# Hybrid Mamba-2 and attention trunk: y in 64-token pieces, group 0 turned off TensorE, and a softmax tail moved one group forward

## The chip, the cores and the metric

One core of one Trainium2 chip runs the kernel. The metric is device time in microseconds (us): the median over runs of the same program. A profiled execution shows what each engine of the core did: PE (TensorE matmuls) and PEld (its weight loads), DVE (VectorE), ACT (ScalarE), POOL (GpSimd) and SP, whose queue starts most DMAs. An "L" and a number is a line of the kernel.

## The reference

Two layers over 256 tokens of width 2048, each followed by a layer norm of the input (times a constant) plus the layer's output. The first layer is a Mamba-2 state-space mixer with 64 heads of 64 in 8 groups, the second a sliding-window attention with 32 query heads over 4 shared key/value heads. The part of the first layer that the change touches, cut from the reference:

```python
zxbcdt = x @ w_in                       # z, xbc, dt_raw
xbc = silu(causal_conv4(xbc) + conv_b)  # xs (64 heads of 64), bm and cm (8 groups of 128)
dt = softplus(dt_raw + dt_bias); a = -exp(a_log)
da_cum = cumsum(dt * a)                 # per head, over tokens
cb     = einsum("bcqgn,bcsgn->bgcqs", c, b)                        # C with B, per group
y_diag = einsum("bgcqs,bgrcqs,bcsgrp->bcqgrp", cb, exp(segsum(da)), xs * dt)
# (the reference cuts tokens into chunks of 128 and carries states between them)
y = y_diag + y_off + xs * d_skip
y = rmsnorm_per_group(y * silu(z)) * norm_w
out = y @ w_out
```

For query token q and earlier token s, the weight of a head is cb[q, s] times the exponential of the sum of da between s and q. In the attention layer, scores become weights by a softmax over the window with one sink per head, the weighted values are multiplied by silu(gate), and an output projection follows.

## The kernel before

**Weights.** All large products are in float32, split in two parts: `wr` is a weight tile from memory (128x1024, loaded through SP's queue into six buffers), ScalarE makes its high part `wh` (L178), VectorE the rest `wl` (L181), and TensorE multiplies three times, high by high, high by low, low by high. A block of 128 output columns for 256 tokens is 48 matmuls of 256 columns (L265); a piece of an output projection is 24 matmuls of 512 columns (L339). Four tiles each of `wh` and `wl` go round.

**Layer one.** `_sequence` sets the order of the input blocks, one block a step. A group g has ten blocks: B, C, four `xs` and four `z`. For group 0 three of the `z` come first, then B, C, the four `xs` and the last `z` (`BLOCKS0`, steps 0 to 9); steps 10 to 19 are group 1's in the plain order. After a block's product, ScalarE and VectorE do the convolution: `cv` by ScalarE (L508), three more taps by VectorE (L510), then tanh by ScalarE (L515) and a product by VectorE (L516), which gives `bt`, `ct` or `xs`. Output pieces of an earlier group lie between the blocks (`OUT_AT`). Tables (`plan`, `beside`, `between`, filled by `at`) say at which step every small operation is written; a scheduler with priorities may shift it, except what is pinned to the written order. Each engine then works its own list in order.

**A group's y.** Tokens stand on the partitions as the earlier token s, in two blocks c of 128. The heads are worked in two halves of four, hf.

- `load_decay` fetches the running sums of da for four heads (`rb`), copied to all partitions, by one DMA per half. `sum_decay` forms the differences: per head one ScalarE operation of 256 and one of 128 columns (L566), since the second token block needs only the later 128 queries. `exp_decay` takes the exponential of all 1536 columns (L573).
- `cb` multiplies B with C for the whole group in two matmuls (L607, L608), and VectorE masks the result (L609). `by_cb` multiplies the exponentials of a half by it (L614). This product is `e`.
- `xd` holds xs times dt with tokens on partitions. For groups 1 to 7 VectorE transposes xs in 32x32 blocks (`turn_xs`, L641), ScalarE copies the blocks to their places (`carry_xs`, 16 copies, L651) and VectorE multiplies by dt (`scale_xs`, L657). For group 0 `turn_first` does it: eight TensorE transposes (L625) and four VectorE products out of PSUM (L629).
- `ymm` (L659) forms y: 16 matmuls for a group, each over 128 tokens s, 64 rows of output and 256 or 128 queries. Two heads go to the two halves of the output rows. TensorE works each float32 matmul as two records in the trace, so there are 32 records per group. VectorE takes y out of PSUM (L675, L681), POOL multiplies by the gate (L686, `gate`).

**Layer two.** `B_ORDER` gives the order of the query blocks q, gate blocks g and output blocks o for the four key/value heads j. After each half h of a group's attention, `weigh` (L1252 to L1255: sums, reciprocal, product) and `turn_far` (a VectorE transpose `z`, L1262, then 16 ScalarE copies, L1281) turn the scores into weights. They are called `rest`: for the two halves listed in `BEHIND_HALF` they are put off, (1, 1) to a later point in the next attention half, and (3, 0) to behind the first gate `sg` of block g3 (`behind_gate`). All others run at once. The gate is ScalarE's tanh (L1185) and VectorE's product (L1186), which frees the PSUM tile of the gate block; four `mm` tiles of PSUM go round.

Of the kernel before, what the change touches and what calls it, by code (L numbers as in the profile page):

```python
# [17 lines left out]
P = 128  # L18
S = 256
# [51 lines left out]
NSM = 7  # L71
B_ORDER = [("q", 0), ("g", 0), ("q", 1), ("g", 1), ("q", 2), ("o", 0), ("g", 2), ("q", 3),
# [6 lines left out]
BEHIND_HALF = [(1, 1), (3, 0)]  # L79
# [18 lines left out]
def trunk(ctx: ExitStack, tc: tile.TileContext, A: dict, out: bass.AP, dbg=None):  # L98
# [30 lines left out]
    mask_ssd = cc[:, 256:640]  # L129

    tri = cc[:, 256:384]
# [60 lines left out]
    def load_first():  # L192

        us = [new_unit([WHOLE, WHOLE]) for _ in range(NF)]
        raws = []
        for tag, n in FIRST:
            if tag == "xr":
                buf = xr_t
            elif tag == "wr":
                buf = wp.tile([P, 1024], F32, tag="wr", name=nm("first"), bufs=NR)  # L200
            else:
                w, bufs = {"rb": (1024, 2), "e": (1536, 2), "yz": (1024, 1)}[tag]
# [211 lines left out]
    dtx = ap.tile([P, 2, NHD], F32, tag="dtx", name="dtx")  # L414
    rtk = ap.tile([P, 2, 2 * NHD], F32, tag="rtk", name="rtk")
# [68 lines left out]
    def turn_dt(sums, dt, q):  # L484
        pt = ax_tile()
        for i, v in enumerate((sums[:, 0, :], sums[:, 1, :], dt)):
            nc.tensor.transpose(pt[:, i * P : (i + 1) * P], v, ident)
        nc.scalar.copy(
            rtk[:].rearrange("p c (k h) -> p k c h", k=2),
            pt[:, :256].rearrange("p (k c h) -> p k c h", k=2, c=2),  # L490
        )
        elo = q[:]
        nc.scalar.activation(
            elo[:, :128].rearrange("p (c h) -> p c h", c=2), rtk[:, :, 64:128], AF.Exp, scale=-1.0
        )
        nc.vector.tensor_tensor(
            dtx[:], pt[:, 256:384].rearrange("p (c h) -> p c h", c=2),
            elo[:, :128].rearrange("p (c h) -> p c h", c=2), ALU.mult,
# [30 lines left out]
    def load_decay(g, hf):  # L529
        rb = ap.tile([P, 4, S], F32, tag="rb", name=nm("rb"), bufs=2)  # L530
# [3 lines left out]
        m = (nc.sync if sp else nc.gpsimd).dma_start(  # L534
            rb[:],
            rscr[h0 : h0 + 4, :]
            .rearrange("h q -> (h q)").partition_broadcast(P)
            .rearrange("p (h q) -> p h q", h=4),
        )
        if sp and g < 2:  # L540
            tc.keep_in_program_order(m)
        rbs[g, hf] = rb
# [13 lines left out]
    def sum_decay(g, hf, first=0, last=4):  # L556

        rb = rbs[g, hf]
        h0 = g * 8 + hf * 4
        if first == 0:  # L560
            es[g, hf] = ap.tile([P, 4, 384], F32, tag="e", name=nm("e"), bufs=2)
        e = es[g, hf]
        for h in range(first, last):
            for c, cols in ((0, slice(0, 256)), (1, slice(256, 384))):
# [6 lines left out]
    def exp_decay(g, hf):  # L571
        e = es[g, hf]
        m = nc.scalar.activation(e[:], e[:], AF.Exp, scale=-1.0)  # L573
# [29 lines left out]
    def cb(g):  # L603
        st = gs[g]
        cbm = ap.tile([P, 384], F32, tag="cbm", name=nm("cbm"), bufs=1)
        ps = ax_tile()
        nc.tensor.matmul(ps[:, :256], st.bt[:, :128], st.ct[:], start=True, stop=True)  # L607
        nc.tensor.matmul(ps[:, 256:384], st.bt[:, 128:], st.ct[:, 128:], start=True, stop=True)  # L608
        nc.vector.tensor_tensor(cbm[:], ps[:, :384], mask_ssd, ALU.mult)  # L609
        st.cbm = cbm  # L610

    def by_cb(g, hf):
        e = es[g, hf]
        nc.vector.tensor_tensor(e[:], e[:], gs[g].cbm[:].unsqueeze(1).to_broadcast([P, 4, 384]), ALU.mult)  # L614

    def turn_first(g):

        st = gs[g]
        st.xd = ap.tile([P, 2, 4, P], F32, tag="xd", name=nm("xd"), bufs=1)
        for k in range(2):  # L620
            ps = ax_tile()
            for i in (2 * k, 2 * k + 1):
                for c in range(2):
                    o = (i % 2) * S + c * P
                    nc.tensor.transpose(ps[:, o : o + P], st.xs[i][:, c * P : (c + 1) * P], ident)  # L625
            for i in (2 * k, 2 * k + 1):
                o = (i % 2) * S
                hh = g * 8 + 2 * i
                m = nc.vector.tensor_tensor(  # L629
                    st.xd[:, :, i, :].rearrange("p c (h d) -> p c h d", h=2),  # L630
                    ps[:, o : o + S].rearrange("p (c h d) -> p c h d", c=2, h=2),
                    dtx[:, :, hh : hh + 2].unsqueeze(3).to_broadcast([P, 2, 2, 64]), ALU.mult,
                )
                pinned(m, True)

    def turn_xs(g):
# [3 lines left out]
        for i in range(4):  # L640
            m = nc.vector.transpose(st.zx[:, i].rearrange("p f b -> p (f b)"), st.xs[i][:])  # L641
            pinned(m, g == 1)
        st.xd = ap.tile([P, 2, 4, P], F32, tag="xd", name=nm("xd"), bufs=1)

    def carry_xs(g, js):

        st = gs[g]
        z = st.zx[:].rearrange("p i (c j) b -> p j c i b", c=2)
        for j in js:
            for i in range(4):  # L650
                m = nc.scalar.copy(st.xd[32 * j : 32 * j + 32, :, :, 32 * i : 32 * i + 32], z[32 * i : 32 * i + 32, j])  # L651
                pinned(m, g > 1 and j > 1)

    def scale_xs(g):
        v = gs[g].xd[:].rearrange("p c i (h d) -> p c (i h) d", h=2)
        d = dtx[:, :, g * 8 : g * 8 + 8].unsqueeze(3).to_broadcast([P, 2, 8, 64])
        pinned(nc.vector.tensor_tensor(v, v, d, ALU.mult), g == 0)  # L657

    def ymm(g):  # L659
        st = gs[g]  # L660
        st.yz = ap.tile([P, 4, S], F32, tag="yz", name=nm("yz"), bufs=1)
        for k in range(2):
            ps = ax_tile()
            for i in (2 * k, 2 * k + 1):
                o = (i % 2) * S
                for c in range(2):
                    cols = slice(o + c * P, o + S)
                    for r in range(2):
                        e = es[g, i // 2][:, 2 * (i % 2) + r, :]
                        nc.tensor.matmul(  # L670
                            ps[64 * r : 64 * r + 64, cols], st.xd[:, c, i, 64 * r : 64 * r + 64], e[:, 256:] if c else e[:, :256],
                            start=c == 0, stop=c == 1,
                        )
            two = slice(2 * k, 2 * k + 2)
            nc.vector.tensor_tensor(  # L675
                st.yz[:, two, :], ps[:].rearrange("p (i q) -> p i q", i=2), els[g][:, two, :], ALU.mult
            )
            for i in (2 * k, 2 * k + 1):
# [90 lines left out]
    visits = (turn_dt, cb, turn_first, ymm, norm)  # L769
# [89 lines left out]
    for g in range(NG):  # L859
        t = FIRST_XS[g]  # L860
        if g == 0:
# [5 lines left out]
            between[11] = [(turn_first, 0)]  # L867
# [55 lines left out]
        for i in range(4):  # L923
# [269 lines left out]
    def attend(j, h):  # L1193
# [172 lines left out]
        if (j, h) in BEHIND_HALF:  # L1366
            (behind_gate if j == 3 else halves).append(rest)
# [120 lines left out]
def _layout(inputs):  # L1488
# [61 lines left out]
    cc[:, 256:384] = tri  # L1550
    cc[:, 384:512] = 1.0
    cc[:, 512:640] = tri
# [31 lines left out]
```

## Time and profile before

| | |
|---|---|
| device time, median of 3 runs | 975.44 us (975.06 to 976.07) |
| profiled execution: time, and its span | 975.83 us, 973.8 us |
| PE busy | 965.5 us (99%) |
| DVE busy | 786.6 us (81%) |
| ACT busy | 671.4 us (69%) |
| POOL busy | 119.1 us (12%) |
| granted TensorE clock | 1.00 in every stretch |

The span is the time from the first to the last record; 2.03 us of the profiled execution lie outside it. Busy shares are averages over the whole span. A group's mean duration is that of one instruction, and neighbours on an engine can overlap by up to a tenth of a microsecond, so that the distance from start to start is shorter than a duration.

### The profile page before, as it was taken

To read this page: it belongs to the slowest core of one execution; us is meant where nothing else is said; L and a number is where in the kernel's file an instruction comes from. 1 tells how busy PE (TensorE), PEld (TensorE's weight loads), DVE (VectorE), ACT (ScalarE), POOL (GpSimd) and SP (SyncE) were. 2 spreads that over 40 slices of the span, in tenths; PEclk is the share of its full clock that TensorE was granted. 3 is DMA by queue.
4 is the path that set the end of the run, shared out by engine and by line. 5 is a ranking of instruction groups with operands and counts; after the bars stand their busy time and mean duration, and the time that the engine had idled before them with its cause. 6 is when DMAs were issued, how large, how long until landed. Compare 5 with 4: busy or idle time off the path is not lost.

```text
span 973.8 us, 18857 instructions
## 1 busy us (share of the span) xinstructions
PE 965.5 (99%) x7332; PEld 892.0 (92%) x7332; DVE 786.6 (81%) x1217; ACT 671.4 (69%) x1282; POOL 119.1 (12%) x202
## 2 busy tenths in 40 slices
PE   9999999999999999999999999999999999999998
PEld 8999989998999999999899899888999988898976
DVE  7978898896977877787797687889977769778778
ACT  7675884884785686487477579467777776884772
POOL 0000403102110310310300121411000000000002
PEclk9999999999999999999999999999999999999999
DMA  9689467676656666576476654568654545456542
GB/s 359 237 290 337 147 216 228 212 230 203 218 192 220 205 205 206 167 237 213 152 250 203 216 178 155 187 190 265 193 174 158 185 138 186 153 177 213 205 143 86
DMA packets 61273, 197.90 MB, mean 203 GB/s; under 512 B 6800, under 2 KB 11328, under 8 KB 60928
## 3 DMA queue, kind: packets, MB, share of 16 engines
q1 hardware_dynamic: 58528, 188.53, 59.1%
q0 software_dynamic: 2048, 7.65, 2.4%
q8 instruction: 57, 0.93, 0.4%
q10 hardware_dynamic: 608, 0.52, 0.2%
q14 instruction: 32, 0.26, 0.1%
HBM read 194.45 MB, written 2.23 MB: 202 GB/s over the span
## 4 chain that ended last, share of the span: by engine, by line
PE 75%; DVE 10%; ACT 6%; DMA 5%; issue 3%; SPq 1%; DVEq 0%; ACTq 0%
PE mm L265 48%; PE mm L339 20%; DVE wl L181 4%; DMA wr<-in_wa 2%; PE mm L1052 2%; PE ax L670 2%; ACT wh L178 2%; DMA wr<-in_wb 1%; ACT p L1248 1%; DMA xr<-in_first 1%; DVE cv L510 1%; ACT e L566 1%; ACT ptw L1281 1%; ACT pt L1281 0%; DMA rscr<-f 0%
## 5 line engine op out<-in xcount | busy, mean ns | idle before, releaser
L181 DVE TENSOR_TENSOR wl<-wr,wh 128x1024 fp32r<-128x1024 f32 (+2 forms) x354 | 391.5, 1126 | 87.8 <-ACT wh L178 86.0
L178 ACT ACTIVATE wh<-wr 128x1024 fp32r<-128x1024 f32 (+2 forms) x354 | 332.9, 974 | 95.9 <-PE mm L265 50.9
L265 PE MATMUL mm<-xH,wh 128*128 128x256 f32 x1280 | 354.6, 277 | 0.1
L265 PE MATMUL mm<-xH,wl 128*128 128x256 f32 x1280 | 353.8, 276 | 0.0
L265 PE MATMUL mm<-xL,wh 128*128 128x256 f32 x1280 | 353.7, 276 | 0.0
L265 PEld LDWEIGHTS mm<-xH,wh 128*128 128x128 f32 x1280 | 240.3, 188 | 2.3 <-issue 1.0
L265 PEld LDWEIGHTS mm<-xL,wh 128*128 128x128 f32 x1280 | 240.4, 188 | 1.0
L265 PEld LDWEIGHTS mm<-xH,wl 128*128 128x128 f32 x1280 | 240.3, 188 | 0.1
L265 PE MATMUL mm<-x1H,wh 128*128 128x256 f32 x512 | 142.2, 278 | 2.1 <-DVE sg L1186 2.1
L265 PE MATMUL mm<-x1L,wh 128*128 128x256 f32 x512 | 141.6, 277 | 0.0
L265 PE MATMUL mm<-x1H,wl 128*128 128x256 f32 x512 | 141.5, 276 | 0.0
L339 PE MATMUL mm<-wh,yH 128*128 128x512 f32 x256 | 100.8, 394 | 0.1
L339 PE MATMUL mm<-wh,yL 128*128 128x512 f32 x256 | 99.8, 390 | 0.0
L339 PE MATMUL mm<-wl,yH 128*128 128x512 f32 x256 | 99.7, 390 | 0.0
L265 PEld LDWEIGHTS mm<-x1H,wh 128*128 128x128 f32 x512 | 96.1, 188 | 3.6 <-DVE sg L1186 2.4
L265 PEld LDWEIGHTS mm<-x1L,wh 128*128 128x128 f32 x512 | 96.2, 188 | 0.1
L265 PEld LDWEIGHTS mm<-x1H,wl 128*128 128x128 f32 x512 | 96.2, 188 | 0.0
L510 DVE SCALAR_TENSOR_TENSOR cv<-mm,pc,cv 128x255 f32<-128x255 f32 x144 | 68.4, 476 | 4.6 <-ACT cv L508 2.5
L686 POOL TENSOR_TENSOR yz<-yz,z 128x256 f32<-128x256 f32 x32 | 26.7, 843 | 259.2 <-DVE yz L681 259.2
L339 PEld LDWEIGHTS mm<-wl,yH 128*128 128x128 f32 x256 | 48.1, 188 | 10.3
L339 PEld LDWEIGHTS mm<-wh,yH 128*128 128x128 f32 x256 | 48.1, 188 | 9.7 <-issue 0.3
L339 PEld LDWEIGHTS mm<-wh,yL 128*128 128x128 f32 x256 | 48.1, 188 | 9.0
(247 smaller groups left out, 1262.8 us busy)
## 6 DMA issues: line engine op xcount, KB each, us to landing
wr<-in_wa SPq DMA_DIRECT2D x154, 512.0 KB, 5.2
wr<-in_wo SPq DMA_DIRECT2D x64, 512.0 KB, 4.4
wr<-in_wq SPq DMA_DIRECT2D x32, 512.0 KB, 4.4
wr<-in_wg SPq DMA_DIRECT2D x31, 512.0 KB, 4.8
wr<-in_wb SPq DMA_DIRECT2D x16, 512.0 KB, 4.0
wr<-in_wb SPq DMA_DIRECT2D x32, 256.0 KB, 4.3
rb<-rscr SPq DMA_DIRECT2D x11, 512.0 KB, 5.4
wr<-in_wkv SPq DMA_DIRECT2D x8, 512.0 KB, 5.7
```

The lines of the kernel that those rows point to most:

```text
L178: m = nc.scalar.activation(h[:, sl], v, AF.Copy)
L181: m = nc.vector.tensor_tensor(l[:, sl], v, h[:, sl].bitcast(F32), ALU.subtract)
L265: m = nc.tensor.matmul(ps, a, b, start=first and i == 0, stop=last and i == 2)
L339: pinned(nc.tensor.matmul(ps, a[:, k, hs], (u.h, u.l)[l][:, ks], start=n == 0 and add is None, stop=n == 11), pin)
L510: nc.vector.scalar_tensor_tensor(a[:, sft:], ps[:, : S - sft], w(3 - sft), a[:, sft:], ALU.mult, ALU.add)
L566: m = nc.scalar.activation(e[:, h, cols], rb[:, h, c * P :], AF.Relu, scale=-1.0, bias=rtk[:, c, h0 + h : h0 + h + 1])
L670: nc.tensor.matmul(ps[64 * r : 64 * r + 64, cols], st.xd[:, c, i, 64 * r : 64 * r + 64], e[:, 256:] if c else e[:, :256], start=c == 0, st ...
L686: nc.gpsimd.tensor_tensor(v, v, st.z[i][:], ALU.mult)
L1052: m = nc.tensor.matmul(ps[:], (x1H, x1L, x1H)[i][:, kk, hs], (u.h, u.h, u.l)[i][:, ks], start=(kk, i) == (0, 0), stop=ui == 3 and (k, i) = ...
L1248: nc.scalar.activation(byhead[:, r], byhead[:, r], AF.Exp, bias=ng[:, r : r + 1], accum_out=rs[:, r : r + 1])
L1281: nc.scalar.copy(to[32 * c : 32 * c + 32].rearrange("p r a -> p (r a)"), src[32 * i : 32 * i + 32, cc_].rearrange("p r b -> p (r b)"),)
```

## The change

**The y product in 64-token pieces.** A group's earlier tokens are now cut in four pieces of 64. For piece c only queries from 64c on are needed, so the widths are 256, 192, 128 and 64 (`PART` gives their places in `e`). Tokens of one piece stand on half of the partitions: row half r holds one set of heads and the other half another, and b chooses the half of the output rows. `ymm` issues 32 matmuls, each over 64 tokens and 64 output rows, in sets of four that use the four quadrants of the array. `e` has 1280 columns for a half in place of 1536, and its PSUM tiles are one per row half. `cb` becomes four matmuls of 256, 192, 128 and 64 columns into output row halves, VectorE masks them in two operations of 64x320, and POOL copies both to the other half of the partitions (two copies more). `load_decay` fetches only the two heads that a row half needs: two DMAs of half the size for each before, in a buffer of their own kind; `sum_decay` has still 16 operations per group, of 256, 192, 128 and 64 columns; `turn_dt` copies in four pieces.

```diff
-        nc.tensor.matmul(ps[:, :256], st.bt[:, :128], st.ct[:], start=True, stop=True)
-        nc.tensor.matmul(ps[:, 256:384], st.bt[:, 128:], st.ct[:, 128:], start=True, stop=True)
-        nc.vector.tensor_tensor(cbm[:], ps[:, :384], mask_ssd, ALU.mult)
+        for c, half, to in ((0, 0, 0), (1, 64, 0), (2, 64, 192), (3, 0, 256)):
+            nc.tensor.matmul(
+                ps[half : half + 64, to : to + 256 - 64 * c], st.bt[:, 64 * c : 64 * c + 64], st.ct[:, 64 * c :],
+                start=True, stop=True,
+            )
+        for r in range(2):
+            rows, at = slice(64 * r, 64 * r + 64), slice(320 * r, 320 * r + 320)
+            nc.vector.tensor_tensor(cbm[rows, at], ps[rows, :320], mask_ssd[rows], ALU.mult)
+        for r in range(2):
+            ...
+            nc.gpsimd.tensor_copy(cbm[64 - 64 * r : 128 - 64 * r, at], cbm[rows, at])
...
     def ymm(g):
...
+        pss = [ax_tile(), ax_tile()]
         for k in range(2):
-            ps = ax_tile()
-            for i in (2 * k, 2 * k + 1):
-                o = (i % 2) * S
-                for c in range(2):
-                    cols = slice(o + c * P, o + S)
-                    for r in range(2):
-                        e = es[g, i // 2][:, 2 * (i % 2) + r, :]
+            for c in range(4):
+                for r in range(2):
+                    rows = slice(64 * r, 64 * r + 64)
+                    for b in range(2):
                         nc.tensor.matmul(
-                            ps[64 * r : 64 * r + 64, cols], st.xd[:, c, i, 64 * r : 64 * r + 64], e[:, 256:] if c else e[:, :256],
-                            start=c == 0, stop=c == 1,
+                            pss[r][64 * b : 64 * b + 64, k * S + 64 * c : k * S + S], st.xd[rows, k, b, c],
+                            es[g, k][rows, b, PART[c]], start=c == 0, stop=c == 3,
                         )
...
     def load_decay(g, hf):
-        rb = ap.tile([P, 4, S], F32, tag="rb", name=nm("rb"), bufs=2)
+        rb = ap.tile([P, 2, 2, S], F32, tag="rb", name=nm("rb"), bufs=2)
...
+        for r in range(2):
+            m = (nc.sync if sp else nc.gpsimd).dma_start(
+                rb[64 * r : 64 * r + 64, 0],
...
     def sum_decay(g, hf, first=0, last=4):
...
+            for c in range(4):
                 m = nc.scalar.activation(
-                    e[:, h, cols], rb[:, h, c * P :], AF.Relu, scale=-1.0, bias=rtk[:, c, h0 + h : h0 + h + 1]
+                    e[:, b, PART[c]], rbs[g, hf][:, b, 64 * c :], AF.Relu, scale=-1.0,
+                    bias=rtk[:, c % 2, 0, c // 2, n : n + 1],
```

**Group 0's xs.** `turn_first` is gone. `turn_xs`, `carry_xs` and `scale_xs` do for group 0 what they do for the others, at steps 9, 10 and 11; `ymm` of group 0 stays behind step 13. The gates of a group go in the order 0, 2, 1, 3.

```diff
-            between[11] = [(turn_first, 0)]
+            at(9, turn_xs, 0)
+            at(10, carry_xs, 0, (0, 1))
+            at(11, carry_xs, 0, (2, 3))
+            at(11, scale_xs, 0)
...
-        for i in range(4):
+        for i in (0, 2, 1, 3):
             at(y, gate, g, i)
```

On ScalarE, group 0's exponentials (`e` in place), the block of B of group 1 (`bt`) and the weights of the steps after it stand like this before:

```order
L573 ACTIVATE e_871<-e_871 128x1536
L178 ACTIVATE wh_1091<-wr_1095 128x1024
L178 ACTIVATE wh_1173<-wr_1175 128x1024
L508 ACTIVATE cv_1079<-mm_1029,pc 128x256
L178 ACTIVATE wh_1173<-wr_1177 128x1024
L515 ACTIVATE bt_1078<-cv_1079 128x256
L178 ACTIVATE wh_1241<-wr_1243 128x1024
```

And after the change:

```order
L571 ACTIVATE e_876<-e_876 128x1280
L638 COPY xd_1032<-zx_1027 32x2x4x32 x8
L505 ACTIVATE cv_1095<-mm_1045,pc 128x256
L178 ACTIVATE wh_1117<-wr_1121 128x1024
L638 COPY xd_1032<-zx_1027 32x2x4x32 x6
L512 ACTIVATE bt_1094<-cv_1095 128x256
L638 COPY xd_1032<-zx_1027 32x2x4x32 x2
L178 ACTIVATE wh_1193<-wr_1195 128x1024
L178 ACTIVATE wh_1193<-wr_1197 128x1024
```

Sixteen copies now stand ahead of the weights for the next steps. On VectorE the products that make group 0's `xd` stand behind `bt` of group 1 and ahead of the block of `ct` before:

```order
L516 SCALAR_TENSOR_TENSOR bt_1078<-bt_1078,cv_1079 128x256
L629 TENSOR_TENSOR xd_1150<-ax_1151,dtx 128x2x128 x2
L629 TENSOR_TENSOR xd_1150<-ax_1158,dtx 128x2x128 x2
L510 SCALAR_TENSOR_TENSOR cv_1166<-mm_1101,pc,cv_1166 128x255
L181 TENSOR_TENSOR wl_1242<-wr_1243,wh_1241 128x1024
```

And after, with five `wl` products and the whole of `ct` (group 1's C, step 11) in between:

```order
L513 SCALAR_TENSOR_TENSOR bt_1094<-bt_1094,cv_1095 128x256
L181 TENSOR_TENSOR wl_1194<-wr_1195,wh_1193 128x1024
L181 TENSOR_TENSOR wl_1194<-wr_1197,wh_1193 128x1024
L507 SCALAR_TENSOR_TENSOR cv_1177<-mm_1127,pc,cv_1177 128x255
L181 TENSOR_TENSOR wl_1262<-wr_1263,wh_1261 128x1024
L507 SCALAR_TENSOR_TENSOR cv_1177<-mm_1127,pc,cv_1177 128x254
L181 TENSOR_TENSOR wl_1262<-wr_1265,wh_1261 128x1024
L507 SCALAR_TENSOR_TENSOR cv_1177<-mm_1127,pc,cv_1177 128x253
L181 TENSOR_TENSOR wl_1402<-wr_1403,wh_1401 128x1024
L513 SCALAR_TENSOR_TENSOR ct_1176<-ct_1176,cv_1177 128x256
L647 TENSOR_TENSOR xd_1032<-xd_1032,dtx 128x1024
```

The one product `scale_xs` (L647 after) moved behind `ct`; TensorE's `ymm` of group 0 reads its result and stands behind step 13 in both kernels.

**The softmax tail.** The tail of the half (2, 0) is put off behind the first gate of block g2, and the tail of (3, 0) runs at once.

```diff
-BEHIND_HALF = [(1, 1), (3, 0)]
+BEHIND_HALF = [(1, 1), (2, 0)]
...
-            (behind_gate if j == 3 else halves).append(rest)
+            (behind_gate if j == 2 else halves).append(rest)
```

On VectorE, around the first gate of g2 (`sg_9891`, its PSUM tile `mm_9904`), the steps of `weigh` and the transpose `z` stand ahead of it before:

```order
L181 TENSOR_TENSOR wl_9960<-wr_9961,wh_9959 128x896
L1252 TENSOR_TENSOR sm_9821<-sm_9821 128x8
L1253 RECIPROCAL sm_9821<-sm_9821 128x8
L1254 TENSOR_SCALAR sm_9821<-sm_9821 128x8
L1255 TENSOR_TENSOR p_9808<-p_9808,sm_9821 128x8x4x32
L181 TENSOR_TENSOR wl_9960<-wr_9963,wh_9959 128x1024
L1262 STREAM_TRANSPOSE z_9839<-p_9808 128x1024
L1186 SCALAR_TENSOR_TENSOR sg_9891<-sg_9891,mm_9904 128x256
```

And behind it after (the gate is `sg_10080`, its PSUM tile `mm_10093`):

```order
L181 TENSOR_TENSOR wl_10151<-wr_10152,wh_10150 128x896
L181 TENSOR_TENSOR wl_10151<-wr_10154,wh_10150 128x1024
L1178 SCALAR_TENSOR_TENSOR sg_10080<-sg_10080,mm_10093 128x256
L1244 TENSOR_TENSOR sm_10016<-sm_10016 128x8
L181 TENSOR_TENSOR wl_10290<-wr_10291,wh_10289 128x128
L1245 RECIPROCAL sm_10016<-sm_10016 128x8
L181 TENSOR_TENSOR wl_10290<-wr_10291,wh_10289 128x896
L1246 TENSOR_SCALAR sm_10016<-sm_10016 128x8
L181 TENSOR_TENSOR wl_10290<-wr_10293,wh_10289 128x1024
L1247 TENSOR_TENSOR p_10003<-p_10003,sm_10016 128x8x4x32
L1254 STREAM_TRANSPOSE z_10148<-p_10003 128x1024
```

The gate moved ahead of the four `weigh` steps and the transpose; the `wl` products of the next weight tile stand among them.

More of the change, by code (lines that the diff above doesn't have):

```diff
@@ L411, in first_products @@
         return pss
-    dtx = ap.tile([P, 2, NHD], F32, tag="dtx", name="dtx")
-    rtk = ap.tile([P, 2, 2 * NHD], F32, tag="rtk", name="rtk")
+    dtx = ap.tile([P, NHD // 2, 4], F32, tag="dtx", name="dtx")
+    rtk = ap.tile([P, 2, 3, 2, NHD // 2], F32, tag="rtk", name="rtk")
     rscr = dram.tile([P, S], F32, tag="rscr", name="rscr")
@@ L613, in by_cb @@
         e = es[g, hf]
[L614 to L620, printed above, removed]
-            ps = ax_tile()
-            for i in (2 * k, 2 * k + 1):
-                for c in range(2):
-                    o = (i % 2) * S + c * P
-                    nc.tensor.transpose(ps[:, o : o + P], st.xs[i][:, c * P : (c + 1) * P], ident)
-            for i in (2 * k, 2 * k + 1):
-                o = (i % 2) * S
[L628 to L634, printed above, removed]
+        nc.vector.tensor_tensor(e, e, gs[g].cbm[:].unsqueeze(1).to_broadcast([P, 2, 640]), ALU.mult)
     def turn_xs(g):
```

88 lines of the change are left out of this document (42 added, 46 removed).

## The prediction

> **What bounds the kernel now.** I read the page's busy times first, then who keeps TensorE waiting, then stretches of the span, and last the rows around the three places that the change touches.
>
> The page's first part (busy time, share of the span, instructions) and the waits of TensorE over the whole span (engine, line, what it waited for, us, times, longest):
>
> ```profile
> PE 965.5 (99%) x7332; PEld 892.0 (92%) x7332; DVE 786.6 (81%) x1217; ACT 671.4 (69%) x1282; POOL 119.1 (12%) x202
> PE mm L265 <- DVE sg L1186: 2.1, 1, 2.1
> PE ax L724 <- POOL sq L692: 0.3, 1, 0.3
> ```
>
> TensorE is the bound: 99% busy, and one wait of 2.1 us is the largest. The same by stretches (length, then busy us and records of PE, PEld, DVE, ACT, POOL, the granted clock, DMA):
>
> ```profile
> 60.00:88.00 28.00, 28.00 (x251) 27.73 (x251) 25.13 (x37) 20.04 (x34) 1.06 (x2) 1.00 0.86 316
> 88.00:130.00 42.00, 41.74 (x324) 38.87 (x319) 36.57 (x59) 28.50 (x50) 11.42 (x15) 1.00 0.57 184
> 130.00:142.00 12.00, 11.86 (x78) 10.22 (x76) 9.82 (x12) 11.80 (x21) 0.00 (x0) 1.00 0.62 196
> 142.00:784.00 642.00, 642.00 (x4938) 601.27 (x4938) 518.90 (x755) 447.18 (x793) 96.56 (x167) 1.00 0.63 202
> 784.00:836.00 52.00, 49.84 (x359) 43.24 (x360) 42.06 (x71) 36.78 (x91) 0.00 (x0) 1.00 0.51 161
> ```
>
> From 142 to 784 us TensorE never stops, so there a microsecond of its work is a microsecond of the time. From 60 to 88 it does not stop either, but VectorE works 25.13 of 28 us: little has to go wrong there. The profiled execution took 975.83 us (973.8 of span, 2.03 around it), 0.39 above the median of 975.44. I sum against 975.83 and take 0.39 off. About 0.2%, 1.95 us, is what a measurement of this kernel can tell from no change.
>
> **Term 1: y in 64-token pieces.** The matmuls of y (L670) and the only ones that use four quadrants, the scores L1220 (duration min/median/max, first and last start, shapes); then TensorE's busy time of one visit of each, 32 records both:
>
> ```profile
> L670 PE MATMUL ax<-e,xd x256: 272/326/430, 87.4 to 613.2; 128*64 128x256 f32 x64, 128*64 128x128 f32 x64
> 87.00:91.00 4.00, 2.82 (x32) 2.00 (x32) 1.00 0.98 355
> L1220 PE MATMUL ax<-kT,qT x128: 322/323/373, 733.3 to 906.2; 64*64 64x192 f32 x128
> 733.00:735.00 2.00, 1.53 (x32) 1.13 (x32) 1.00 0.81 262
> ```
>
> L670 has 16 records of 256 and 16 of 128 columns, two side by side: 8x256 + 8x128 = 3072 column steps in 2.82 us. L1220 has eight sets of four: 8x192 = 1536 steps in 1.53. The difference gives 0.84 ns a step, and 0.24 us is left for filling. That this fits one price shows that four quadrants do run side by side. After, 64 records make 16 sets, four each of 256, 192, 128 and 64: 2560 steps, 2.15 + 0.24 = 2.39 us, or 0.43 less. The trace has no set as short as 64 columns. Its lower bound is 0.054 us, its upper one the shortest step the trace has, 128 columns or 0.108: four times 0.054 more, a gain of only 0.21. I take 0.35, nearer the first, because loads overlap: 32 loads of 133 ns each fill only 1.13 us. Eight groups: -2.8 us (-1.7 to -3.4).
>
> The page "TensorE: Matmul & The Clock Gate" of the Trainium skill (LDWEIGHTS) puts a weight load at its columns over 1.2, in ns, that is 53 for 64 columns; four in a row would be an estimated 0.21 us a set, 16 sets 3.4 us, and the change a loss of 0.8 a group. The trace disagrees with loads in a row: a set of L1220 takes 0.161 with four loads.
>
> **Term 2: B with C.** The chain of waits around a y visit and around a `cb` that stands alone (start, us, what, records):
>
> ```profile
> 142.02 2.75 PE ax L670 x32
> 144.77 5.66 PE mm L339 x24
> 177.66 0.43 PE ax L607 x2
> 178.10 0.22 PE ax L608 x2
> 178.32 10.90 PE mm L265 x96
> 189.22 5.46 PE mm L339 x24
> ```
>
> `cb` alone costs 0.65 us, and the blocks behind it run at their plain pace. Now it works in 64-column halves. Side by side they have 320 columns each, 2x320x0.84 = 0.54 us, 0.11 less. But a visit in halves disturbs: L670 takes 2.75 for 2.58 us of steps, and the 24 records behind it 5.66 instead of 5.46: 0.37 in all. So a `cb` alone costs +0.26 (0 to +0.5). That counts for groups 1 and 2: +0.5. Group 0's lies at 58 us, ahead of the wait of term 3, which swallows it. For groups 3 to 7 `cb` follows a y visit that pays this already: I take 0. "TensorEngine Tiling (Array Packing)" of the Trainium skill (Key Properties) says that a change of tiling mode drains the TensorE, and y and `cb` now differ in it. By half of the 0.37 for each of five visits the sum would be 0.9 higher; the trace has `cb` only without a change of mode.
>
> VectorE's mask goes from one operation to two and POOL gets two copies per group. `e` has 1280 columns for 1536, which saves VectorE and ScalarE time. From 142 on that is hidden, since no wait of TensorE comes from them. Doubled DMA issues with half the bytes: hidden too, SP only feeds tiles ahead of use.
>
> **Term 3: group 0's xs.** This is on TensorE's path from 87 us on. Rows of what goes (L625, L629), and of what takes its place in later groups (L641, L651, L657); the last is who VectorE's L657 waited for:
>
> ```profile
> L625 PE MATMUL ax<-cc,xs x8: 272/272/273, 75.5 to 76.3; 128*128 128x128 f32 x8
> L629 DVE TENSOR_TENSOR xd<-ax,dtx x4: 415/416/418, 81.5 to 82.5; 128x256 f32<-128x256 f32 x4
> L651 ACT COPY xd<-zx x112: 387/403/408, 127.3 to 604.2; 32x256 f32<-32x256 f32 x112
> L657 DVE TENSOR_TENSOR xd<-xd,dtx x7: 1226/1226/1226, 137.4 to 604.7; 128x1024 f32<-128x1024 f32 x7
>   ACT xd L651: 12.5, 7
> ```
>
> Before, xd is ready at 82.9 (82.5 + 0.4) and y starts at 87.4: 4.5 us of slack. After, 16 copies of 0.40, 6.5 us, enter ScalarE's list ahead of weights that VectorE waits for. Timelines of ScalarE, then VectorE, before (start, us, line, names, shapes):
>
> ```profile
> 72.65 1.47 ACT L573 ACTIVATE e<-e 128x1536 f32<-128x1536 f32 x1
> 74.02 1.99 ACT L178 ACTIVATE wh<-wr 128x1024 fp32r<-128x1024 f32 x2
> 75.92 0.54 ACT L508 ACTIVATE cv<-mm,pc 128x256 f32<-128x256 f32 x1
> 76.36 1.04 ACT L178 ACTIVATE wh<-wr 128x1024 fp32r<-128x1024 f32 x1
> 80.71 0.42 ACT L515 ACTIVATE bt<-cv 128x256 f32<-128x256 f32 x1 [3.30 <-DVE cv L510]
> 74.15 1.76 DVE L614 TENSOR_TENSOR e<-e,cbm 128x1536 f32<-128x1536 f32 x1
> 83.22 1.22 DVE L181 TENSOR_TENSOR wl<-wr,wh 128x1024 fp32r<-128x1024 f32 x1
> 84.35 0.48 DVE L510 SCALAR_TENSOR_TENSOR cv<-mm,pc,cv 128x254 f32<-128x254 f32 x1
> 84.74 1.22 DVE L181 TENSOR_TENSOR wl<-wr,wh 128x1024 fp32r<-128x1024 f32 x1
> 86.90 0.43 DVE L516 SCALAR_TENSOR_TENSOR ct<-ct,cv 128x256 f32<-128x256 f32 x1 [0.54 <-ACT ct L515]
> ```
>
> From start to start a `wh` takes 0.95 and a `cv` 0.44 on ScalarE, a `wl` 1.13 and a `cv` 0.39 on VectorE. ScalarE after, in its new order: the exponential (1280 columns, 5/6 of 1.47) ends at 73.9. Eight copies (3.2) bring it to 77.1, `cv` and a `wh` to 78.5, eight copies and a tanh (0.4) to 82.1, and the next `wh` to 83.1. Only then can VectorE go on with the first of the five `wl` ahead of `scale_xs`: five `wl`, three `cv` and `ct` (0.43), together 7.3, to 90.4, and L657 itself 1.2: xd at 91.6. TensorE would be ready at about 86.5 (87.4 less the transposes of 75.5 to 76.3). So it stands for 5 us, and y starts at 91.6 instead of 87.4: **+4.2**. Lower bound: if VectorE never waited for ScalarE, the second half's L614 ends at 75.6 (5/6 of 1.76 from 74.15), seven `wl`, six `cv`, `bt` and `ct` take 11.1, L657 1.2: 87.9, +0.5. Upper bound: the largest idle that ScalarE caused on L657 later is 12.5 over seven, 1.8 each, on top: +6. I take 4.2, since the lists are fixed and the copies have no other place. TensorE works its list in order, so all behind y waits too. ScalarE and VectorE gain lead meanwhile, so the 0.40 us that TensorE stands from 88 to 142 should shrink: -0.3 (0 to -0.4).
>
> **Term 4: the softmax tail.** VectorE's timeline ahead of the 2.1 us wait, and the tanh of the same gate:
>
> ```profile
> 831.12 0.17 DVE L1252 TENSOR_TENSOR sm<-sm 128x8 f32<-128x8 f32 x1 [1.49 <-ACT p L1248]
> 831.76 1.23 DVE L1255 TENSOR_TENSOR p<-p,sm 128x1024 f32<-128x1024 f32 x1
> 832.90 1.22 DVE L181 TENSOR_TENSOR wl<-wr,wh 128x1024 fp32r<-128x1024 f32 x1
> 834.04 1.24 DVE L1262 STREAM_TRANSPOSE z<-p 128x1024 f32<-128x1024 f32 x1
> 835.20 0.38 DVE L1186 SCALAR_TENSOR_TENSOR sg<-sg,mm 128x256 f32<-128x256 f32 x1
> 832.14 0.36 ACT L1185 ACTIVATE sg<-mm 128x256 f32<-128x256 f32 x1
> ```
>
> The gate sits behind `weigh` and `z` and frees the tile that TensorE wants. After, only the `wl` stands ahead of it; that can start at about 832.0, and the gate at 833.1, when its tanh has long ended (832.5). It ends at 833.5, when TensorE arrives (835.6 less 2.1). Gain 2.0 (1.7 to 2.1). `weigh` and its `wl` neighbours come later, and the tile after next needs the second gate: 0 to 0.3 us there. Put back to at once, the tail of (3, 0) delays g3's first gate by about 2 us, but that tile is wanted only four tiles later.
>
> **Sum:** 975.83 + 4.2 - 0.3 - 2.8 + 0.5 - 2.0 = 975.4, less 0.39: **975.0**. No change that can be told: three gains and one loss of like size.
>
> **Rivals.**
>
> - *No stall at group 0's y.* VectorE finds its weights ready, as in the lower bound of term 3 (+0.5). For it: ScalarE is busy for only 20.04 of 28 us there, so 6.5 us more fit. Against: they are bunched ahead of `wh`. Then 975.0 - 3.7 = **971.3**, faster.
> - *Short sets are no faster than sets of 192* (slower). Place: every y visit. Price: 4x0.215 + 12x0.161 + 0.24 = 3.03 us a visit, +0.21 instead of -0.35, over eight groups +4.5: **979.5**. It decides if sets of 64 and 128 columns stand more than about 0.13 us apart. For it: no shorter set is in the trace. Against: L670's pairs of 128 columns take 0.108.
> - *A new hold of VectorE from 107 to 131.* POOL must now copy group 1's mask product, and in POOL's list these copies stand behind DMA issues that wait for ScalarE; VectorE's `by_cb` waits for them, and `wl` products queue behind it. I price it at 2 us, the largest wait TensorE has now: **977.0**.
> - *The tail's wait does not go*, or comes back at the next tile: +2.0, also **977.0**.
>
> **How the numbers follow.** Forecast 0.45 (its own range 973.0 to 977.0; of it 0.16 below 973.5, 0.24 within 0.2%, 0.05 above 977.4). No stall 0.20, faster. Short sets 0.14, slower. VectorE's hold 0.11 (0.03 same, 0.08 slower), the tail 0.10 (0.04 same, 0.06 slower). Together 0.36 faster, 0.31 same, 0.33 slower. The range 971.0 to 979.2 leaves out parts of the two outer cases, some 0.18.
>
> **What would show it.** In the profile after: TensorE's waits name the L647 product of group 0 with some 5 us (term 3) and no longer the gate (term 4); a y visit of 64 records is busy for 2.4 to 2.5 us (term 1); a `cb` alone takes 0.5 to 0.6 with a slower block behind it (term 2). A first y record near 88, a y visit over 2.8, or a wait behind POOL's copies would prove me wrong.

## The result, and the profile after

The changed kernel takes 981.98 us (median of 4 runs, 981.89 to 982.84); before takes 975.26 (4 runs, 975.06 to 976.07). The ratio is 1.0069, 95% interval 1.0055 to 1.0084: 6.7 us slower, where I had forecast no change and a range to 979.2. The profiled execution after took 981.89 us, with a span of 980.1.

The page's first part and the waits of TensorE over the span, after:

```profile
PE 967.0 (99%) x7612; PEld 895.2 (91%) x7612; DVE 789.4 (81%) x1226; ACT 671.8 (69%) x1301; POOL 124.3 (13%) x223
PE ax L658 <- DVE xd L647: 4.0, 1, 4.0
PE mm L339 <- DVE xr L350: 1.9, 1, 1.9
PE mm L339 <- DVE sg L1178: 0.5, 1, 0.5
```

The gate of g2 no longer stands among the waits with 2.1 us. In its place are 4.0 us at group 0's y (L658 is the y matmul now, L647 `scale_xs`), and 1.9 us at a tile of an output piece that VectorE empties (L350). TensorE's busy time rose by 1.5 us, although y has a sixth fewer column steps. The stretches of before, after the change, with the first one behind y split finely (length, busy of PE, PEld, DVE, ACT, POOL, granted clock, DMA):

```profile
60.00:88.00 28.00, 28.00 (x238) 28.00 (x239) 21.86 (x33) 25.16 (x48) 2.96 (x6) 1.00 0.75 243
90.00:92.00 2.00, 0.00 (x0) 0.00 (x0) 2.00 (x3) 2.00 (x4) 0.00 (x0) 0.76 0.96 315
92.00:94.00 2.00, 1.56 (x19) 1.22 (x23) 2.00 (x4) 0.54 (x1) 0.00 (x0) 0.50 1.02 389
94.00:96.00 2.00, 2.00 (x36) 1.67 (x32) 1.96 (x4) 1.18 (x3) 0.00 (x0) 0.50 1.03 373
96.00:98.00 2.00, 2.00 (x28) 1.84 (x21) 1.92 (x4) 0.64 (x1) 0.00 (x0) 0.53 0.94 322
98.00:100.00 2.00, 2.00 (x20) 2.00 (x19) 1.97 (x5) 1.10 (x2) 0.00 (x0) 1.00 0.72 242
142.00:784.00 642.00, 642.00 (x5180) 604.47 (x5179) 521.19 (x762) 442.53 (x789) 97.84 (x179) 1.00 0.62 198
784.00:836.00 52.00, 51.91 (x381) 44.65 (x383) 39.99 (x65) 37.22 (x94) 0.00 (x0) 1.00 0.52 167
836.00:904.00 68.00, 65.75 (x504) 58.70 (x496) 53.65 (x86) 45.21 (x104) 0.00 (x0) 1.00 0.56 183
```

From 60 to 88 us ScalarE went from 20.04 to 25.16 us busy and VectorE from 25.13 down to 21.86: it waits for ScalarE. In the wait for xd the granted clock falls to one half, and the whole y visit and the start of the next block run at it, until about 98 us. From 836 to 904 TensorE stands for 2.25 us; before it worked all 68.

Both kernels have the same 6636 matmuls of the large products in the same order, so TensorE's lag against before can be read at each of them from the start times of the two traces:

| matmul, us before | lag after, us | what lies between it and the row above |
|---|---|---|
| 59.07 | +0.80 | the start, group 0's `cb` |
| 76.29 | +0.64 | three blocks; the transposes are gone |
| 90.12 | +6.80 | the wait for xd and group 0's y at half clock |
| 144.70 | +5.52 | group 1's `cb` and y; the profile of before is slow here (see below) |
| 236.22 | +5.79 | group 2's `cb` |
| 613.37 | +3.94 | five y visits |
| 835.64 | +2.03 | the gate of g2 |
| 879.37 | +4.87 | the wait for xr |
| 954.09 | +5.92 | the later gates and output pieces |

The profile of before is itself one execution. From 90.12 to 144.70 us it takes 54.58 us; the two later profiles in which only the softmax tail differs from before take 53.15 each for the same matmuls. So the fall from 6.80 to 5.52 is no gain of the change, and a microsecond in this table can be chance.

### The profile page after: what moved, and what is told of

The parts are those of the page before. It is cut to its first block, busy times and chain, and to the rows that moved or that the text cites. A ratio compares the mean times of both kernels' runs of the same rounds, so it can differ in the third digit from the quotient of the medians.

```text
span 980.1 us, 19514 instructions
## 1 busy us (share of the span) xinstructions
PE 967.0 (99%) x7612; PEld 895.2 (91%) x7612; DVE 789.4 (81%) x1226; ACT 671.8 (69%) x1301; POOL 124.3 (13%) x223
## 4 chain that ended last, share of the span: by engine, by line
PE 78%; DVE 8%; ACT 7%; DMA 4%; issue 3%; ACTq 0%; SPq 0%; DVEq 0%
PE mm L265 48%; PE mm L339 23%; DVE wl L181 3%; PE mm L1044 2%; ACT wh L178 2%; PE ax L658 2%; DMA wr<-in_wa 2%; ACT p L1240 1%; DMA xr<-in_first 1%; ACT pt L1273 1%; ACT xd L638 1%; DMA wr<-in_wb 1%; DVE cv L507 1%; ACT ptw L1273 1%; DVE z L1254 1%
## 5 line engine op out<-in xcount | busy, mean ns | idle before, releaser
L689 ACT ACTIVATE yH<-yz,pc 128x256 fp32r<-128x256 f32 x32 | 16.3, 510 | 69.7 <-POOL yz L675 69.7
```

The source lines that it names most:

```text
L689: nc.scalar.activation(yH[:, i, :], v, AF.Copy, scale=pc[:, c : c + 1])
```

## The experiments

Times of a run are compared with runs of before on the same chip (975.15 to 975.24 in all of them).

**One edit undone or done alone.** First the tail, as before, in the changed kernel:

```diff
-BEHIND_HALF = [(1, 1), (2, 0)]   # behind_gate if j == 2
+BEHIND_HALF = [(1, 1), (3, 0)]   # behind_gate if j == 3
```

> The changed kernel with the softmax tail as before: (3, 0) put off, (2, 0) at once. Theory: moving the tail saved the 2.1 us wait at the first gate of g2 (TensorE's lag against before falls from 3.9 to 2.0 us there) and gave back 3.9 us between 860 and 955 us, because VectorE and ScalarE did weigh, the transpose and the sixteen copies later and ran behind from then on. Undone, the 2.1 us wait is back, the wait for xr L350 (1.9) is gone, and the time is 982.0 - 3.9 + 1.9 = 980.0. Rival: the late waits come from the start or from the smaller pieces; then they stay, the 2.1 us wait comes on top, and the time is about 984.

Measured: 978.13 us (6 runs, 977.28 to 980.15), ratio 1.0036 (1.0023 to 1.0049). Its waits, and the granted clock behind y:

```profile
PE ax L658 <- DVE xd L647: 3.3, 1, 3.3
PE mm L265 <- DVE sg L1178: 2.1, 1, 2.1
92.00:94.00 2.00, 2.00 (x61) 1.86 (x54) 1.96 (x4) 0.15 (x1) 0.00 (x0) 1.00 1.00 391
```

The wait at the gate is back and the one for xr is gone, as expected, but the time fell by 3.9 and not by 2. In this profile the wait for xd had no halved clock behind it. So I ran the changed kernel again:

> The changed kernel once more, beside the others on one chip, since the same wait for xd stood with the clock at a half in one profile (lag behind before 6.8 us at the block after y) and without in another (3.7). Theory: the halved clock follows the wait in most executions and costs about 2.5 us there; the time is 982 again, with single runs between 979.5 and 983. Rival: it was chance in the first profile, and the median is near 979.5.

Measured: 980.83 us (4 runs, 979.32 to 981.95), ratio 1.0054 (1.0039 to 1.0069); the clock fell again in its profile (0.55 from 92 to 94 us) after a wait of only 2.4 us. Whether the clock halves differs between executions, and the four times go from 979.32 us at a mean clock of 0.998 to 981.95 at 0.996. This lies between theory and rival. Against this second measurement, undoing the tail is worth 2.7 us and not 3.9.

Then group 0's xs turned on TensorE in the changed kernel, and the same with the tail as before:

```diff
-            at(9, turn_xs, 0) ... at(11, scale_xs, 0)
+            between[11] = [(turn_first, 0)]
+    # turn_first: for a, c, r: nc.tensor.matmul(ps[64 * r : 64 * r + 64, c * P : c * P + P],
+    #     st.xs[2 * a + r][:, 64 * c : 64 * c + 64], ident), then one VectorE product with dtx per a
```

> The changed kernel, with group 0's xs turned on TensorE again: sixteen matmuls with the identity into 64-row halves at the place of the old transposes, and two VectorE products of 128x512. Theory: the whole of the start's loss comes from the sixteen copies on ScalarE. Then y of group 0 starts without a wait, the clock stays at 1.00; TensorE's lag at 144 us is 5.5 now, and becomes what it was ahead of the copies (0.6) plus 2.1 for the 16 matmuls with their change of shape, less the 0.4 of y and what the later pinch gives back (about 0.5): 1.8. Time 982.0 - 3.7 = 978.3. Rival: the smaller pieces or POOL's copies of the mask product hold VectorE at the start as well; then a wait stays at y, and the time is over 980.

> Both together: group 0 turned on TensorE as in the run before this one, and the tail as before. What is left of the change are the 64-token pieces. Theory: the two losses have nothing to do with each other and add up: 978.3 - 2.0 = 976.3, with the y visits worth 8 x 0.36 = 2.9. Rival: the pieces themselves cost nothing and gain nothing beyond the start; then about 979.

Measured: 977.35 us (9 runs), ratio 1.0021 (1.0011 to 1.0031), and 976.02 us (10 runs), ratio 1.0008 (0.9998 to 1.0017). Neither waits at y: the stall and the clock behind it come with group 0's xs, and without them the tail is worth 1.3 us. That it is ScalarE's list that makes the stall rests on the rows shown under term 3 below. What is left in the second, the pieces, does not gain: eight y visits give 3.0 us, and the slower pace behind B with C (below) takes 1.6, the turning in the new layout 0.9. These would leave a gain of 0.5; the run shows 0.8 more than before, with an interval from -0.2 to 1.7. TensorE's busy time for the turning, in the first of the two and in before:

```profile
75.00:80.00 5.00, 1.97 (x32) 1.73 (x32) 1.00 0.93 306
```

```profile
75.00:77.00 2.00, 1.04 (x8) 0.89 (x8) 1.00 0.87 293
```

At 59 us these two kernels already lag by 0.6 and 1.3 us, of which `cb` makes 0.1. Three profiles that run before's own code up to there lag by 0.2 to 0.5, so part of it is chance; the rest of the start I did not trace to a cause.

The other way round, before with one edit each: only the xs of group 0 (with `turn_xs` pinned for it), and only the tail:

```diff
-            between[11] = [(turn_first, 0)]
+            at(9, turn_xs, 0) ... at(11, scale_xs, 0)
```

> The kernel before with only group 0's xs turned by VectorE and ScalarE, at the steps that the change gives them; pieces, gates and tail as before. Theory: this edit alone makes the stall at group 0's y, 3 to 5 us, and in part of the executions the halved clock behind it: 975.2 + 4.2 - 0.3 = 979.1 without the halved clock, up to 981.6 with it. Rival: the smaller pieces have their share in it (later start, slower pace, POOL's copies ahead of VectorE's by_cb); then it is under 977.

> The kernel before with only the softmax tail changed: (2, 0) put off, (3, 0) at once. Theory: the 2.1 us wait at 835 us goes, ScalarE and VectorE run late from there, and TensorE waits for xr L350 at about 880 us for 1.9 us and loses some 0.5 more at the later gates; as between the two kernels with group 0 turned on TensorE (977.35 and 976.02) it ends 1.3 slower: 976.5. Rival: before has more slack there, since its ScalarE has no POOL copies or smaller pieces behind it; then it gains 2.0: 973.2.

Measured: 980.88 us (4 runs, 979.79 to 981.76), ratio 1.0055 (1.0038 to 1.0072), for the xs; 976.41 us (10 runs), ratio 1.0012 (1.0003 to 1.0022), for the tail. Waits of the first, its stretch behind y, and the wait of the second:

```profile
PE ax L670 <- DVE xd L657: 4.7, 1, 4.7
92.00:94.00 2.00, 2.00 (x14) 1.35 (x13) 1.97 (x4) 0.00 (x0) 0.00 (x0) 0.50 0.88 332
```

```profile
PE mm L339 <- DVE xr L350: 1.9, 1, 1.9
836.00:904.00 68.00, 66.02 (x468) 59.06 (x467) 52.48 (x86) 46.51 (x107) 0.00 (x0) 0.97 0.52 168
```

The xs alone cost 5.7 us, the tail alone 1.2. Together that is 6.9, for a whole of 6.7 (5.6 in the second measurement): the two losses are the result, and the pieces, whose gain was to pay for them, come out near nothing. Behind the 1.9 us wait at xr the clock halved in this profile of the tail alone (the 0.97 is its mean), and in neither profile of the changed kernel; how much of the 1.2 us is the clock's stays open.

**TensorE kept busy in the wait.** Nine matmuls whose result is overwritten, ahead of group 0's y:

```diff
+        for _ in range(9 if g == 0 else 0):
+            tc.keep_in_program_order(nc.tensor.matmul(pss[0][:, :256], ident, cc[:, 256:512], start=True, stop=True))
```

> The changed kernel with nine matmuls of 128x128x256 more, whose result is overwritten, put ahead of group 0's y, where TensorE stood for 4.0 us; they take 9 x 0.43 = 3.9 us and are done when xd is. They leave the wait for xd as it is and take away only TensorE's idle time. Theory: the halved granted clock from 91 to 97.5 us came from the idle time. Then the clock stays at 1.00, the y visit takes 2.4 instead of 4.5 us, and the time is 982.0 - 2.5 = 979.5. Rival: the clock has another cause, or what it costs is waited for anyway; then the time stays at 982.

Measured: 983.37 us (4 runs, 981.39 to 983.91), ratio 1.008 (1.0065 to 1.0095): no gain. The profile is that of the fastest of the four. Its stretches and a new wait, the nine matmuls, and VectorE's first operation that takes y out of PSUM, here and (last row) in the changed kernel:

```profile
88.00:92.00 4.00, 4.00 (x24) 3.64 (x23) 4.00 (x7) 2.77 (x4) 0.00 (x0) 1.00 0.93 286
92.00:98.00 6.00, 6.00 (x93) 5.26 (x92) 5.85 (x9) 1.82 (x3) 0.00 (x0) 1.00 0.95 360
PE ax L715 <- POOL sq L683: 1.4, 1, 1.4
88.84 4.05 PE L654 MATMUL ax<-cc 128*128 128x256 f32 x18
98.98 1.28 DVE L666 TENSOR_TENSOR yz<-ax,el 128x512 f32<-128x512 f32 x2
```

```profile
98.72 0.68 DVE L664 TENSOR_TENSOR yz<-ax,el 128x512 f32<-128x512 f32 x1
```

The clock stayed at 1.00 here. That agrees with the theory and does not prove it, since the changed kernel with the tail undone kept its clock with a wait of 3.3 us in place. The fill was also too long: xd was ready at 91.6 us, and the nine matmuls ended at 92.9. And the clock is not all that holds what follows. VectorE comes to y at 98.98 us here and at 98.72 in the changed kernel, although y ends 1.8 us earlier here; TensorE then stood for 1.4 us at the sums of the norm (L715), which need y after VectorE and POOL. From 87 to 110 us its lag grows by 4.7 us here and by 5.9 in the changed kernel, so about half of the 2.2 us that the clock cost at y was saved. Part of what the clock costs is waited for anyway, as the rival said. Why the other three runs took 2 us more than the profiled one is not known.

**The copies on POOL.** POOL is nearly idle there; with the tail as before, the sixteen copies went to it, and `scale_xs` to ahead of the convolution of step 11:

```diff
-                m = nc.scalar.copy(
+                m = (nc.gpsimd.tensor_copy if g == 0 else nc.scalar.copy)(
...
-            at(10, carry_xs, 0, (0, 1)); at(11, carry_xs, 0, (2, 3)); at(11, scale_xs, 0)
+            at(10, carry_xs, 0, (0, 1, 2, 3)); between[11] = [(scale_xs, 0)]
```

> The changed kernel with the tail as before, with group 0's sixteen copies on POOL, which is idle there, and with its scale_xs written ahead of the convolution of step 11. Theory: the stall at group 0's y was ScalarE's list and the place of scale_xs behind ct. Then xd is ready near 82, TensorE does not wait and keeps its clock, and against the same kernel with the copies on ScalarE (978.1) 3.3 us go: 974.8. Rival: VectorE is short of time there in any case, or POOL's copies are slow; then a wait of over 1 us stays and the time is over 976.

Measured: 982.83 us (4 runs, 980.47 to 984.04), ratio 1.0073 (1.0056 to 1.0089). The profile is that of the slowest of the four. POOL's copies (with their shortest, median and longest in ns), VectorE's wait for them, and TensorE's:

```profile
75.62 10.63 POOL L638 COPY xd<-zx 32x256 f32<-32x256 f32 x16
L638 POOL COPY xd<-zx x16: 392/396/1565, 75.6 to 85.8; 32x256 f32<-32x256 f32 x16
86.28 1.23 DVE L647 TENSOR_TENSOR xd<-xd,dtx 128x1024 f32<-128x1024 f32 x1 [5.17 <-POOL xd L638]
PE ax L713 <- POOL sq L681: 8.9, 1, 8.9
```

The stall at y is gone, and worse stands 20 us later. `scale_xs` held VectorE for 5.17 us, everything in its list behind it came later, y out of PSUM too, and TensorE waited 8.9 us at the sums of the norm. What held VectorE between 60 and 110 us was paid at y in the changed kernel and at the norm here. The run moved the copies and `scale_xs` together, so it does not tell the two apart.

**A full-width matmul behind B with C.** The same kernel with one matmul more behind the four of groups 0 and 2:

```diff
+        if g in (0, 2):
+            tc.keep_in_program_order(nc.tensor.matmul(ps[:, 384:512], ident, cc[:, 256:384], start=True, stop=True))
```

> As the run before this one, with one matmul of 128x128x128 more (identity by a constant, into a part of the tile that nothing reads) behind the four 64-column matmuls of B with C of groups 0 and 2. In all profiles with the smaller pieces the 256-column matmuls that follow such a visit come 0.118 us apart instead of 0.113, for 240 and 96 of them, until the next visit or output piece: 1.6 us. Theory: what follows takes its pace from the shape of the last matmuls ahead of it; a full-width one brings 0.113 back: 1.6 less for 0.4 of work, 974.8 - 1.2 = 973.6. Rival: the pace has another cause (what VectorE and ScalarE do meanwhile); then it stays at 0.118 and the time is 0.4 longer than without, 975.2.

Measured: 981.98 us (4 runs, 981.30 to 983.37), ratio 1.0071 (1.0055 to 1.0088). The expected 973.6 built on the 974.8 that the run before had missed, and 0.85 us less than that run is within the scatter. The chain around group 2's `cb` in the changed kernel, then here (start, us, records):

```profile
183.23 0.69 PE ax L606 x6
183.92 11.51 PE mm L265 x96
```

```profile
184.30 0.69 PE ax L606 x6
184.99 0.42 PE ax L611 x2
185.41 10.90 PE mm L265 x96
```

Before has 10.90 there too. With the full-width matmul between, the 96 records are back at the plain pace: the pace does hang on what ran just before. In the kernel that has no stall:

> The smaller pieces with group 0 turned on TensorE and the tail as before (976.0), and behind B with C of groups 0 and 2 the one full-width matmul. Theory: the slow pace of 0.118 us for 240 and 96 matmuls is a cost of the pieces that the forecast had not; it goes, 1.6 us, for 0.4 of work: 974.8. Rival: in a kernel without a long stall the pace is hidden behind VectorE; then it stays near 976.

Measured: 975.60 us (11 runs), ratio 1.0008 (0.9996 to 1.0020): 0.4 less than without it, which is within the scatter, not the 1.2 expected, and no different from before. The pace is back (10.90), but TensorE waits 0.6 us for VectorE's `cv` in that profile.

**Half of the tail's edit.** Only `turn_far` of (2, 0) behind the gate, in that kernel and in before:

```diff
+        elif (j, h) == (2, 0):
+            weigh()
+            behind_gate.append(turn_far)
```

> The same, with only turn_far of (2, 0) put off behind the gate of g2; weigh runs at once, and (3, 0) is as before. Theory: what made the moved tail lose was the delay of weigh and its weights by some 5 us; the transpose alone in front of the gate costs 1.2 of the 2.1 us wait, and putting off only that delays the sixteen copies by 0.4 us, too little to be waited for. Then 974.8 - 1.2 = 973.6. Rival: any delay of the copies comes back at 880 us, as before; then 974.8 or more.

> The kernel before with only turn_far of (2, 0) put off behind the gate of g2. Theory as in the run before this one: 975.2 - 1.2 = 974.0. Rival: the wait only moves: 975.2.

Measured: 975.64 us (11 runs), ratio 1.0006 (0.9997 to 1.0015), and 975.47 us (11 runs), ratio 1.0006 (0.9997 to 1.0015). The waits of the second:

```profile
PE mm L265 <- DVE sg L1186: 1.4, 2, 0.9
PE mm L339 <- DVE xr L350: 0.6, 1, 0.6
```

The 2.1 us became 0.9 at the first gate, 0.5 at a second one and 0.6 at xr: 2.0 in all. The rival holds: the wait only moves. No version I ran beats before.

## Why the prediction was wrong

**Term 4 failed in its sign: the tail.** The wait of 2.1 us went, as forecast (lag down by 1.9 at 835 us). The step that failed is "`weigh` and its `wl` neighbours come later ... 0 to 0.3 us there". ScalarE and VectorE before (first two rows) and after (the rest; start, us):

```profile
835.31 4.14 ACT L1281 COPY pt<-z 32x256 f32<-32x256 f32 x10 [1.03 <-DVE z L1262]
868.29 0.45 ACT L1169 ACTIVATE qT<-mm,qb 128x256 f32<-128x256 f32 x1
```

```profile
842.62 3.31 ACT L1273 COPY pt<-z 32x256 f32<-32x256 f32 x8 [3.87 <-DVE z L1254]
846.62 0.69 DVE L1350 TENSOR_TENSOR oL<-o,oH 128x512 fp32r<-128x512 f32 x1 [2.87 <-ACT oH L1349]
873.38 0.46 ACT L1161 ACTIVATE qT<-mm,qb 128x256 f32<-128x256 f32 x1
883.51 0.68 DVE L350 TENSOR_TENSOR xr<-xr,mm 128x512 f32<-128x512 f32 x1
```

The copies start 7.3 us later on a TensorE that lags by 2.0; VectorE then waits 2.87 us behind them for `oH`. (The moved half has ten such copies, not sixteen.) The next half, its own twenty copies and the evacuation of `qT` stay about 5 us late, and with them the weights, until VectorE empties the output piece late at 883. I had asked which tile waits next, and not whether ScalarE and VectorE could make up the delay before TensorE needs them. I read TensorE's 2.1 us as the slack of that chain. That the move loses is shown by the runs that differ in the tail alone (1.2 and 1.3 us lost); the reading as slack is borne out by the half tail, which moved the wait and kept its sum. Of the rivals, the last came nearest: the wait came back, though not at the next tile but 45 us later.

**Term 3 had the mechanism and missed what stands behind it: the clock.** ScalarE's list after, and VectorE's:

```profile
74.10 3.30 ACT L638 COPY xd<-zx 32x256 f32<-32x256 f32 x8
78.97 2.52 ACT L638 COPY xd<-zx 32x256 f32<-32x256 f32 x6
82.79 2.01 ACT L178 ACTIVATE wh<-wr 128x1024 fp32r<-128x1024 f32 x2
83.88 2.36 DVE L181 TENSOR_TENSOR wl<-wr,wh 128x1024 fp32r<-128x1024 f32 x2 [1.50 <-ACT wh L178]
90.73 0.42 DVE L513 SCALAR_TENSOR_TENSOR ct<-ct,cv 128x256 f32<-128x256 f32 x1
91.07 1.22 DVE L647 TENSOR_TENSOR xd<-xd,dtx 128x1024 f32<-128x1024 f32 x1
```

I had the `wh` end at 83.1, `scale_xs` at 90.4 and y at 91.6; they are 83.8, 91.07 and 92.44. The sum along fixed lists was right to 0.8 us. It had y 4.2 us late; it is 5.0. The price of the wait was not: I took it at its length. The y visit at half clock takes 4.55 us instead of 2.34, and the lag behind it is 6.80 where a visit at full clock would have left about 4.7. The 0.3 us that I took off for the pinch behind it cannot be read from the fall of the lag to 5.52 at 144, since before's own code gains as much there in other executions. Alone, the edit cost 5.7 us, against 3.9 in my sum.

The halving followed the wait for xd in three of four profiles that had it (4.0, 2.4 and 4.7 us, not 3.3). "TensorE: Matmul & The Clock Gate" of the Trainium skill (Part 1, "What's actually happening") has the clock fall to 4/8 after an idle window of some 3.4 us, counted in windows that run freely. The traces agree with the half and with the windows: within each trace the changes of the clock lie whole multiples of 3.41 us apart. They do not agree on the idle time, since a wait of 2.4 us was enough here, and in the kernel with the tail as before the clock from 836 to 841 us, behind the 2.1 us wait at the gate, fell to 0.66 too.

All fourteen profiles together have 18 waits of TensorE of 1.87 us or more. Apart from the first and last few microseconds of a span, the half clock stands behind 11 of them and nowhere else: behind all four of 4.0 us and more, and behind 7 of the 14 from 1.87 to 3.3. Length does not part these 14 (2.07 us with and without, 3.3 without), but place does: with a raster of 3.41 us laid through the clock's changes in the same trace, the 7 waits that lie whole within one interval have the half clock behind them, and the 7 that a border cuts (one of them by only 0.04 us) do not. This is read from the traces; no run shifted a wait on purpose. That every wait of about 2 us can cost clock I had not weighed.

**Term 1 was right.** A y visit after, and the chain around it:

```profile
147.00:151.00 4.00, 2.41 (x64) 1.99 (x64) 1.00 0.84 269
147.96 2.34 PE ax L658 x64
```

Forecast 2.39 us busy, measured 2.41; the lag falls by 0.37 per visit (5.79 to 3.94 over five). Sets of 64 columns are as fast as their columns, so that rival is out. These five visits have `cb` beside y, so the change of mode between the two, 0.9 us for the five outside my sum, costs nothing that shows. The rival of a new hold of VectorE from 107 to 131 us is out too: TensorE has no wait there in the changed kernel.

**Term 2 had the size in this kernel, by another mechanism.** The visit itself costs 0.69 for 0.65. What I had not priced is the pace behind it: 11.51 us for 96 records that took 10.90, all of it behind group 2's. That makes 0.7 us where I had 0.5, so the size is partly luck. Behind group 0's, 240 records come 0.118 instead of 0.113 us apart, another 1.0 us. The wait for xd swallows that, as forecast: it makes TensorE late at y, and is one reason why it stands 4.0 and not 5 us there. Without the wait, as in the kernels with group 0 turned on TensorE, the full 1.6 us is paid.

**What that leaves.** With the terms as measured alone, the tail is 3.2 us worse than in the sum (+1.2 for -2.0), group 0's xs 1.8 (+5.7 for +3.9), and terms 1 and 2 miss by 0.2 in opposite directions. My sum had 0.4 us of gain, so this makes 4.6 us of loss, of a measured 6.7, or 5.6 the second time. The remaining 1 to 2 us stay open; the lag of 0.8 us at 59 us and the clock are candidates.

## What to carry to other kernels

A wait of the busiest engine can be the slack of a chain on other engines: before taking it away, follow the delayed operations until they have caught up, and look for the next place where TensorE needs them. On engines that work in order, a block of sixteen copies costs what stands behind it in the list, not its own length, and moving it to an idle engine did not help here, with the consumer placed where it had to wait for it. Price an idle time of TensorE of about 2 us or more at its length and, as a chance, the clock that may halve behind it; then ask how much of that the next wait would hide. And take a second profile of the same code before reading a microsecond out of the difference of two.

## What the runs showed of the hardware

The matmuls that follow a visit can keep another pace: 0.118 us apart instead of 0.113 behind four 64-column matmuls, for 240 in a row, and 0.113 again with one full-width matmul between. The sixteen turning matmuls into 64-row halves did not end it (144 records at 0.118 ahead of them, 96 behind). What ran just before is not the whole condition: ten of the fourteen profiles have the slow pace for 108 records near 8 us, long before the first `cb`; before with only the xs edit has it for 144 records behind group 0's y, whose narrowest matmuls have 128 columns, while behind group 0's y in 64-token pieces the block runs at 0.113. Why is not settled. Four quadrants of the array worked side by side down to 64 columns at 0.84 ns a column: a y visit of 2560 column steps took 2.41 us. POOL's copy of 32x256 has the median of ScalarE's, 0.40 us, but single ones took up to 1.57, and sixteen in a row 10.63, where ScalarE's sixteen make 6.6.
